# Layer 1 MLP: the seven products in another order, weights' places released a product later, chunk 1 first at the turn

## The chip, the cores and the metric

The kernel runs on one core of one Trainium2 chip. The metric is the device time of one launch in microseconds (us). A core has TensorE (matmuls, with weight loads in a lane of their own), VectorE (DVE), ScalarE (ACT), GpSimd (POOL) and SyncE (SP, which issues most transfers). Each engine takes its instructions in the order in which the program lists them, and waits at the first one whose operands are not ready.

## The reference, cut to what matters

One inference step of a small two-layer model on 640 tokens (512 latent, 128 context), width 1024. Each layer is a mixer and then an MLP with squared ReLU, whose hidden width is 4096:

```
def squared_relu_mlp(h, w1, w2):
    a = jax.nn.relu(h @ w1)
    return (a * a) @ w2
...
x = x + g2 * squared_relu_mlp(h, w_ff1[l], w_ff2[l])
```

All is float32. The change lies in the MLP of layer 1.

## The kernel before

A float32 product is made of three matmuls of reduced operands: high times high, high times low, low times high (`mm3`, lines 801 to 803). So every operand is split first: ScalarE copies the high half, and VectorE subtracts it from the value, which leaves the low half.

The MLP of layer 1 (`mlp` with `seven`) works with the tokens in two chunks of 320 (`C1`) and the hidden width in eight blocks `b` of four pieces of 128. Blocks 0 and 1 are computed plainly. For blocks 2 to 7, `blocks7` calls `up7(b, p)` twice, for the halves p = 0 and 1 of a block. A half has two pieces of the hidden width, `f` = 2p and `g` = 2p + 1. Two chunks, two halves of the 1024 rows of `w1` and two pieces form a 2x2 by 2x2 matrix product, which `up7` does with seven products in place of eight (the scheme of Strassen and Winograd). Each product is 4 x 3 matmuls of 320 columns. The token-side sums `B[0]` to `B[3]` are made once, in blocks 0 and 1 (`sums`). The weight-side sums are made on the way by `w1s_use`: the raw weights `f0, g0, f1, g1` lie in two raw tiles; for product i ScalarE and VectorE split `src` into a place (lines 558 and 559), and for some i VectorE then repairs a raw piece in place for a later product (line 563).

The seven products go to four PSUM banks, `pa`, `pd`, `pb`, `pc`; three of these are added into a second time. VectorE forms `u2 = p1 + pb` and `u3 = u2 + pd` (line 1581; `p1` is ScalarE's copy of the first `pa`, line 1598). The four results are `g` chunk 1 = `u3 + pc`, `g` chunk 0 = `u2 + pd` after its second product, `f` chunk 1 = `u2 + pc` after its second product, and `f` chunk 0 = `pa` after its second product, a plain sum without VectorE. `finish` then takes relu and square and splits the result into `aa` (lines 1586 to 1589). The program order of these steps in `up7` is written by hand.

After both halves of a block comes the turn to `down` (the product with `w2`). There `cut` first issues the groups of d = 0 and 1 for both chunks with the pieces k = 0 and 1 of the first half alone; then these groups are ended with k = 3 and 2 of the second half, and the other d follow with all four pieces. `residual` (line 1407) adds each group into `x`. Block 7 has a turn of its own with three groups of 384 columns.

The weights have eight places of 128x2x1024 in `Slots`; two are given to `B` when block 1 is done, so six remain. A `w2` piece takes a whole place, a weight of a product half of one, and a place comes back when both of its halves are released (`Weights.free`). `st.pump()` prepares the next weights of a fixed list (14 for the products of a block, then its four `w2` pieces), if a place is free, and does nothing otherwise; this puts the ScalarE copy and the VectorE subtraction (lines 214 and 216 for `w2`) at that point of both engines' program order. In the second half of a block the next weights in the list are the `w2` pieces of the same block. PSUM has six banks for this stage; a new tile takes the one that has been free longest.

Of the kernel before, what the change touches and what calls it, by code (L numbers as in the profile page):

```python
# [12 lines left out]
AF = mybir.ActivationFunctionType  # L13
ALU = mybir.AluOpType
# [122 lines left out]
class Weights:  # L137
# [118 lines left out]
    def free(self, key):  # L256
        del self.tiles[key]
        if key in self.of:
            p = self.of.pop(key)
            if isinstance(p, tuple):  # L260
                p, users, o = p
                users[0] -= 1
                if users[0] or o == 0:
                    return
            self.slots.free.append(p)
# [3 lines left out]
def body(ctx, tc, a):  # L269
    nc = tc.nc  # L270
    mm = nc.tensor.matmul
    act = nc.scalar.activation
    vec = nc.vector
# [21 lines left out]
    st = Weights(nc, rawp)  # L295
# [209 lines left out]
    def tok(t):  # L505
        return slice(t * 128, (t + 1) * 128)
# [41 lines left out]
    def w1s_use(l, b, p, i):  # L548


        def use(ts):
            if i == 0:
                fast[l, b, p] = ts
            ab, cd = (t.rearrange("p (k n) -> p k n", k=4) for t in fast[l, b, p])
            f0, g0, f1, g1 = ab[:, :, 0:128], ab[:, :, 128:256], cd[:, :, 0:128], cd[:, :, 128:256]
            src = (f0, g0, g0, f0, f1, g1, f1)[i]
            w = st.half(("w1s", l, b, p, i)).rearrange("p a (k n) -> p a k n", k=4)
            act(out=w[:, 0], in_=src, func=AF.Copy)  # L558
            vec.tensor_tensor(out=w[:, 1], in0=src, in1=w[:, 0].bitcast(F32), op=ALU.subtract)  # L559
            todo = {0: (g0, f0, g0, ALU.subtract), 1: (g0, g1, g0, ALU.subtract), 2: (f0, g0, f0, ALU.add),  # L560
                    4: (f1, f1, g0, ALU.subtract)}.get(i)
            if todo:
                vec.tensor_tensor(out=todo[0], in0=todo[1], in1=todo[2], op=todo[3])  # L563

        return use
# [197 lines left out]
    for k in range(2):  # L763
# [4 lines left out]
        out=sel, in_=ident.rearrange("p (j q) -> p q j", j=4)[:, 0:2, :], op=ALU.add, axis=AX.X  # L768
# [29 lines left out]
    def mm3(ps, st_, mv, first, last, on=False):  # L798


        mm(ps, lhsT=st_[0], rhs=mv[0], start=first, stop=False, skip_group_check=on)  # L801
        mm(ps, lhsT=st_[0], rhs=mv[1], start=False, stop=False, skip_group_check=on)  # L802
        mm(ps, lhsT=st_[1], rhs=mv[0], start=False, stop=last, skip_group_check=on)  # L803
# [79 lines left out]
    for t in range(NT):  # L883
        p = ps_kv[t][:, 0:RKV]
# [76 lines left out]
    for m in range(3):  # L961
        for c in C0:
            dst, p = qs[:, m, c[0]:c[1]], ps_qa[m, c][:, 0:c[1] - c[0]]
# [88 lines left out]
    for h in range(NH):  # L1052
        q = (new_h(f"qh{h}"), new_h(f"ql{h}"))
        Q.append(q)
        for c in C0:
            n = c[1] - c[0]
            p = psp.tile([128, 512], F32, tag="z", name="q_ps")[:, 0:n]
# [26 lines left out]
    for g in range(8):  # L1084
        p = psp.tile([128, NT, 64], F32, tag="z", name="gm_ps")
# [20 lines left out]
    for i in range(2):  # L1106
        ev = kT[i].rearrange("p (a b) n -> p a b n", b=2)
        nc.gpsimd.dma_start(
            out=ev[64:128, :, 0, :], in_=ckvT[i][64:128, 2, :].unsqueeze(1).to_broadcast([64, NH // 2, NKEY])
        )  # L1110
        nc.gpsimd.dma_start(
            out=ev[0:64, :, 1, :], in_=ckvT[i][0:64, 2, :].unsqueeze(1).to_broadcast([64, NH // 2, NKEY])
        )
    for hp_ in range(NH // 2):
        for c0 in (0, 384):
            p = psp.tile([128, 512], F32, tag="z", name="kT_ps")[:, 0:384]
# [9 lines left out]
            for e in range(2):  # L1126
                r = slice(64 * e, 64 * e + 64)
                hi, lo = (t[r, 2 * hp_ + e, c0:c0 + 384] for t in kT)
# [5 lines left out]
    for j in range(6):  # L1134
        p = psp.tile([128, 512], F32, tag="z", name="v_ps")
# [8 lines left out]
        p = p.rearrange("p (h d) -> p h d", h=NH)  # L1144
# [266 lines left out]
    def bank(nm, n):  # L1411
        return psm.tile([128, 512], F32, tag="m", name=nm)[:, 0:n]
# [34 lines left out]
    def mlp(l, C, H, lead, CL, per_d, per_c, mid, tick=None, turn=None, seven=False):  # L1447
# [107 lines left out]
        def up7(b, p):  # L1555
            n = C[0][1]

            def product(i, op, ps, first):
                w = st.need(("w1s", l, b, p, i))
                if ps is None:  # L1560
                    ps = bank("up_ps", n)
                for k in range(4):
                    r = B[op, k] if isinstance(op, int) else H[op[0]][4 * op[1] + k]
                    mm3(
                        ps, (w[:, 0, tok(k)], w[:, 1, tok(k)]), (r[:, 0, 0:n], r[:, 1, 0:n]),
                        first and k == 0, k == 3, not first,
                    )
                st.free(("w1s", l, b, p, i))
                return ps

            f, g = 2 * p, 2 * p + 1
            rs = {}
            for j in (f, g):
                A[b, j] = fa.tile([128, 2, T], F32R, tag="aa", name="aa")
                rs[j] = fr.tile([128, 2, HW], F32, tag="r", name="r").rearrange("p a n -> p (a n)")

            def new(nm):
                return sc.tile([128, 328], F32, tag="n", name=nm)[:, 0:n]

            def add(out, v, ps):  # L1580
                vec.tensor_tensor(out=out, in0=v, in1=ps, op=ALU.add)

            def finish(j, ci, src=None):
                c = slice(*C[ci])
                r, aa = rs[j][:, c], A[b, j]
                act(out=r, in_=r if src is None else src, func=AF.Relu)  # L1586
                act(out=r, in_=r, func=AF.Square)  # L1587
                act(out=aa[:, 0, c], in_=r, func=AF.Copy)  # L1588
                return lambda: vec.tensor_tensor(  # L1589
                    out=aa[:, 1, c], in0=r, in1=aa[:, 0, c].bitcast(F32), op=ALU.subtract  # L1590
                )

            def out(j, ci):
                return rs[j][:, C[ci][0]:C[ci][1]]

            pa = product(0, (0, 0), None, True)
            p1 = new("p1")
            act(out=p1, in_=pa, func=AF.Copy)
            st.pump()
            pd = product(1, 2, None, True)  # L1600
            st.pump()
            pb = product(2, 1, None, True)
            u2, u3 = new("u2"), new("u3")
            add(u2, p1, pb)
            add(u3, u2, pd)
            st.pump()
            pc = product(3, 0, None, True)
            add(out(g, 1), u3, pc)
            lo = finish(g, 1)
            st.pump()  # L1610
            pa = product(4, (0, 1), pa, False)
            lo()
            lo = finish(f, 0, pa)
            if not p:
                st.pump()
            pd = product(5, 3, pd, False)
            add(out(g, 0), u2, pd)
            lo()
            lo = finish(g, 0)
            pc = product(6, (1, 1), pc, False)  # L1620
            add(out(f, 1), u2, pc)
            lo()
            lo = finish(f, 1)
            lo()
            if not p:
                st.pump()

        def blocks7(f0):

            for b in range(NFB):  # L1630
                if b >= f0:
                    for p in range(FB // 2):
                        up7(b, p)

                cut = (lambda ds, cs: [(d, c, down(b, d, c, None, False, (0, 1))) for c in cs for d in ds])
                if b < f0:
                    for k in (2 * b, 2 * b + 1):
                        bg.add(sums(k, room(k)))
                free = (lambda h: [st.free(("w2", l, b, k, h)) for k in (0, 2)])
                if b < NFB - 1:  # L1640
                    early = cut(range(2), C) if b >= f0 else []
                    todo = [(d, c, None) for d in range(2 if early else 0, KD) for c in C]
                    for j, (d, c, ps) in enumerate(early + todo):
                        ps = down(b, d, c, ps, True, range(FB) if ps is None else (3, 2))
                        residual(ps, d, c, modc[l, 5])
                        bg.step()
                        if j == 7:
                            free(0)
                        if j % 2 or j > 3:
                            st.pump()  # L1650
                    free(1)
                    if b == f0 - 1:
                        bg.drain()
                    continue
                for c in CL:
                    early = cut(range(3), CL[0:1]) if c is CL[0] else []
                    for d in range(KD):
                        if d < len(early):
                            ps = down(b, d, c, early[d][2], True, (3, 2))
                        else:  # L1660
                            ps = down(b, d, c)
                        residual(ps, d, c, modc[l, 5])
                        per_d(c, d)
                    per_c(c)
# [36 lines left out]
        for ci in range(2):  # L1701
            i = 0
            while i < lead:
                n = WIDE[l][ci] if i == 0 else 1
                b, fs = i // FB, [(i + j) % FB for j in range(n)]
# [18 lines left out]
        f1 = lead // FB  # L1724
# [67 lines left out]
    g0 = later_h(0)  # L1792
# [276 lines left out]
    g1 = pool_vec(1)  # L2069
# [117 lines left out]
```

## Time and profile before

| | us |
|---|---|
| median of three runs | 1300.96 |
| lowest, highest | 1296.29, 1301.96 |
| the profiled execution | 1302.88 |
| its span, first to last instruction | 1301.1 |
| TensorE busy | 1261.8 |
| VectorE busy | 826.6 |
| ScalarE busy | 549.3 |

Busy is the sum of an engine's instruction times within the span. The changed code runs from about 959 us to 1265 us of the span. Matmuls overlap one another, so a matmul that lasts 0.31 us can begin 0.147 us after the one before it; a pause shows where starts lie further apart.

### The profile page before, as it was taken

What the parts mean: (1) busy time and instruction counts of PE and PEld (TensorE: products, weight loads), DVE (VectorE), ACT (ScalarE), POOL (GpSimd) and SP (SyncE); (2) the same over time, 40 slices, a digit from 0 to 9 for tenths busy, and PEclk for the clock granted to TensorE, in tenths of its full rate; (3) what the DMA queues carried; (4) which work ended last, traced back from release to release, by engine and by line L of the source; (5) the groups of instructions that cost most, each with busy time, mean ns of one, the idle gap of its engine ahead of it and who ended that gap; (6) DMA issues with size and microseconds to landing.
All of it is one profiled execution on the core that took longest, in us unless ns stands there. A gap on an engine that the chain in (4) does not pass through costs nothing.

```text
span 1301.1 us, 20746 instructions
## 1 busy us (share of the span) xinstructions
PE 1261.8 (97%) x8308; PEld 1183.4 (91%) x8308; DVE 826.6 (64%) x1553; ACT 549.3 (42%) x993; POOL 216.5 (17%) x182
## 2 busy tenths in 40 slices
PE   7999999999999999999999999799999999999997
PEld 5899975689999999999999998789999999999997
DVE  5753864564766575666666638876887567675664
ACT  4445454453453434333343414534235435354353
POOL 0010312221113221313131315610000000000001
PEclk8999999999999999999999999899999999999999
DMA  7742286340335344444353431202113223132102
GB/s 291 261 164 72 81 227 234 131 170 25 116 117 160 113 145 131 150 126 157 119 161 114 147 130 33 97 1 79 52 35 112 80 67 98 38 111 84 61 33 82
DMA packets 63200, 149.89 MB, mean 115 GB/s; under 512 B 5072, under 2 KB 21968, under 8 KB 62592
## 3 DMA queue, kind: packets, MB, share of 16 engines
q1 hardware_dynamic: 61360, 142.53, 33.3%
q0 software_dynamic: 1456, 5.96, 1.9%
q8 instruction: 65, 1.06, 0.3%
q14 instruction: 31, 0.25, 0.1%
q10 hardware_dynamic: 288, 0.08, 0.0%
HBM read 140.02 MB, written 5.39 MB: 112 GB/s over the span
## 4 chain that ended last, share of the span: by engine, by line
PE 79%; DVE 10%; ACT 7%; issue 2%; DMA 1%; POOL 0%; DVEq 0%; ACTq 0%; POOLq 0%
PE dn_ps L802 11%; PE dn_ps L801 11%; PE dn_ps L803 11%; PE up_ps L801 7%; PE up_ps L803 7%; PE up_ps L802 7%; PE wo_ps L801 1%; PE o_ps L1302 1%; PE wo_ps L803 1%; PE wo_ps L802 1%; ACT r L1587 1%; DVE w L216 1%; ACT w L558 1%; ACT r L1586 1%; PE t_ps L1269 1%
## 5 line engine op out<-in xcount | busy, mean ns | idle before, releaser
L801 PE MATMUL dn_ps<-aa,w 128*128 128x320 f32 (+4 forms) x1024 | 319.1, 312 | 2.1 <-ACT aa L1588 2.1
L802 PE MATMUL dn_ps<-aa,w 128*128 128x320 f32 (+4 forms) x1024 | 318.4, 311 | 0.7
L803 PE MATMUL dn_ps<-aa,w 128*128 128x320 f32 (+4 forms) x1024 | 316.8, 309 | 0.0
L802 PE MATMUL up_ps<-h,w 128*128 128x320 f32 (+2 forms) x800 | 248.6, 311 | 6.0 <-DVE h L752 5.9
L801 PE MATMUL up_ps<-h,w 128*128 128x320 f32 (+2 forms) x800 | 249.6, 312 | 1.3 <-ACT h L748 1.3
L803 PE MATMUL up_ps<-h,w 128*128 128x320 f32 (+2 forms) x800 | 248.6, 311 | 0.0
L1407 DVE SCALAR_TENSOR_TENSOR x<-dn_ps,mod,x 128x320 f32<-128x320 f32 (+4 forms) x360 | 144.7, 434 | 115.0 <-PE dn_ps L803 113.2
L801 PEld LDWEIGHTS dn_ps<-aa,w 128*128 128x128 f32 x1024 | 193.1, 189 | 5.8 <-ACT aa L1588 4.1
L216 DVE TENSOR_TENSOR w<-raw,w 128x1024 fp32r<-128x1024 f32 (+4 forms) x122 | 151.3, 1250 | 70.9 <-ACT w L214 69.8
L802 PEld LDWEIGHTS dn_ps<-aa,w 128*128 128x128 f32 x1024 | 193.0, 188 | 2.5 <-DVE aa L1589 2.4
L803 PEld LDWEIGHTS dn_ps<-aa,w 128*128 128x128 f32 x1024 | 193.0, 189 | 0.0
L214 ACT ACTIVATE w<-raw 128x1024 fp32r<-128x1024 f32 (+4 forms) x131 | 132.0, 1026 | 112.0 <-DMA raw<-w_ff 85.0
L802 PEld LDWEIGHTS up_ps<-h,w 128*128 128x128 f32 x800 | 151.2, 189 | 8.1 <-DVE h L752 8.1
L801 PEld LDWEIGHTS up_ps<-h,w 128*128 128x128 f32 x800 | 151.0, 189 | 4.9 <-issue 3.4
L466 POOL TENSOR_TENSOR acc<-acc,raw 128x1024 f32<-128x1024 f32 x42 | 100.7, 2399 | 303.7 <-ACT raw L464 297.6
L803 PEld LDWEIGHTS up_ps<-h,w 128*128 128x128 f32 x800 | 151.0, 189 | 0.0
L559 DVE TENSOR_TENSOR w<-raw,w 128x512 fp32r<-128x512 f32 x84 | 57.7, 687 | 34.6 <-ACT w L558 33.7
L558 ACT ACTIVATE w<-raw 128x512 fp32r<-128x512 f32 x84 | 51.4, 624 | 61.9 <-DVE raw L563 57.1
L464 ACT ACTIVATE raw<-raw,cs 128x1024 f32<-128x1024 f32 x42 | 48.3, 1149 | 62.6 <-DVE acc L459 54.2
L1925 POOL TENSOR_TENSOR y<-y,fg 128x1024 f32<-128x1024 f32 x1 | 2.4, 2392 | 416.5 <-ACT y L1921 416.5
L1481 DVE TENSOR_TENSOR r<-r,up_ps 128x328 f32<-128x328 f32 (+2 forms) x80 | 37.6, 484 | 42.6 <-ACT r L1480 41.0
L1484 DVE TENSOR_TENSOR aa<-r,aa 128x640 fp32r<-128x640 f32 (+3 forms) x52 | 39.6, 762 | 35.6 <-ACT aa L1483 35.6
(404 smaller groups left out, 2122.1 us busy)
## 6 DMA issues: line engine op xcount, KB each, us to landing
raw<-w_ff SPq DMA_DIRECT2D x126, 512.0 KB, 3.6
raw<-w_mod SPq DMA_DIRECT2D x80, 512.0 KB, 3.9
raw<-w_m SPq DMA_DIRECT2D x16, 512.0 KB, 6.0
raw<-w_out SPq DMA_DIRECT2D x8, 512.0 KB, 4.4
kT<-ckvT POOLq DMA_DIRECT2D x4, 768.0 KB, 10.8
xr<-x SPq DMA_DIRECT2D x5, 512.0 KB, 5.5
xs<-x SPq DMA_DIRECT2D x2, 1280.0 KB, 9.3
x<-xs POOLq DMA_DIRECT2D x2, 1280.0 KB, 9.6
```

The costliest lines, as they stand in the source:

```text
L214: self.nc.scalar.activation(out=w[:, 0, 0:size], in_=r, func=AF.Copy)
L216: lo.tensor_tensor(out=w[:, 1, 0:size], in0=r, in1=w[:, 0, 0:size].bitcast(F32), op=ALU.subtract)
L464: act(out=raw if k else acc[1], in_=raw, func=AF.Copy, scale=w[1])
L466: nc.gpsimd.tensor_tensor(out=acc[1], in0=acc[1], in1=raw, op=ALU.add)
L558: act(out=w[:, 0], in_=src, func=AF.Copy)
L559: vec.tensor_tensor(out=w[:, 1], in0=src, in1=w[:, 0].bitcast(F32), op=ALU.subtract)
L801: mm(ps, lhsT=st_[0], rhs=mv[0], start=first, stop=False, skip_group_check=on)
L802: mm(ps, lhsT=st_[0], rhs=mv[1], start=False, stop=False, skip_group_check=on)
L803: mm(ps, lhsT=st_[1], rhs=mv[0], start=False, stop=last, skip_group_check=on)
L1407: vec.scalar_tensor_tensor(out=xv, in0=ps[:, p0:p0 + c1 - c0], scalar=gate[:, d, m:m + 1], in1=xv, op0=ALU.mult, op1=ALU.add)
L1481: vec.tensor_tensor(out=rv, in0=rv, in1=ps, op=ALU.mult)
L1484: vec.tensor_tensor(out=aa[:, 1, lo:hi], in0=r[:, lo:hi], in1=aa[:, 0, lo:hi].bitcast(F32), op=ALU.subtract)
```

## The change

The product that adds into `pa`, the plain sum, goes from fifth to seventh place, and those on `B[3]` (into `pd`) and on chunk 1 (into `pc`) move up to fifth and sixth. `w1s_use` splits the weights in the new order, and the last repair is written to `g0` in place of `f1`. A product's weights are released after the next product has been issued (`gone`) in place of right after it. `finish` of `f` chunk 0, which reads PSUM, squares by a VectorE multiplication of the relu with the PSUM value in place of ScalarE's Square. At the end of the first half `st.pump()` becomes `st.pump(2)`. At the turn, `cut` takes chunk 1 first.

```
--- before.py
+++ after.py
@@ -553,12 +553,12 @@
                 fast[l, b, p] = ts
             ab, cd = (t.rearrange("p (k n) -> p k n", k=4) for t in fast[l, b, p])
             f0, g0, f1, g1 = ab[:, :, 0:128], ab[:, :, 128:256], cd[:, :, 0:128], cd[:, :, 128:256]
-            src = (f0, g0, g0, f0, f1, g1, f1)[i]
+            src = (f0, g0, g0, f0, g1, g0, f1)[i]
             w = st.half(("w1s", l, b, p, i)).rearrange("p a (k n) -> p a k n", k=4)
             act(out=w[:, 0], in_=src, func=AF.Copy)
             vec.tensor_tensor(out=w[:, 1], in0=src, in1=w[:, 0].bitcast(F32), op=ALU.subtract)
             todo = {0: (g0, f0, g0, ALU.subtract), 1: (g0, g1, g0, ALU.subtract), 2: (f0, g0, f0, ALU.add),
-                    4: (f1, f1, g0, ALU.subtract)}.get(i)
+                    4: (g0, f1, g0, ALU.subtract)}.get(i)
             if todo:
                 vec.tensor_tensor(out=todo[0], in0=todo[1], in1=todo[2], op=todo[3])
 
@@ -1555,6 +1555,8 @@
         def up7(b, p):
             n = C[0][1]
 
+            gone = []
+
             def product(i, op, ps, first):
                 w = st.need(("w1s", l, b, p, i))
                 if ps is None:
@@ -1565,7 +1567,10 @@
                         ps, (w[:, 0, tok(k)], w[:, 1, tok(k)]), (r[:, 0, 0:n], r[:, 1, 0:n]),
                         first and k == 0, k == 3, not first,
                     )
-                st.free(("w1s", l, b, p, i))
+
+                gone.append(("w1s", l, b, p, i))
+                if i:
+                    st.free(gone.pop(0))
                 return ps
 
             f, g = 2 * p, 2 * p + 1
@@ -1581,10 +1586,15 @@
                 vec.tensor_tensor(out=out, in0=v, in1=ps, op=ALU.add)
 
             def finish(j, ci, src=None):
+
                 c = slice(*C[ci])
                 r, aa = rs[j][:, c], A[b, j]
-                act(out=r, in_=r if src is None else src, func=AF.Relu)
-                act(out=r, in_=r, func=AF.Square)
+                if src is not None:
+                    act(out=r, in_=src, func=AF.Relu)
+                    vec.tensor_tensor(out=r, in0=r, in1=src, op=ALU.mult)
+                else:
+                    act(out=r, in_=r, func=AF.Relu)
+                    act(out=r, in_=r, func=AF.Square)
                 act(out=aa[:, 0, c], in_=r, func=AF.Copy)
                 return lambda: vec.tensor_tensor(
                     out=aa[:, 1, c], in0=r, in1=aa[:, 0, c].bitcast(F32), op=ALU.subtract
@@ -1608,22 +1618,22 @@
             add(out(g, 1), u3, pc)
             lo = finish(g, 1)
             st.pump()
-            pa = product(4, (0, 1), pa, False)
-            lo()
-            lo = finish(f, 0, pa)
-            if not p:
-                st.pump()
-            pd = product(5, 3, pd, False)
+            pd = product(4, 3, pd, False)
             add(out(g, 0), u2, pd)
             lo()
             lo = finish(g, 0)
-            pc = product(6, (1, 1), pc, False)
+            if not p:
+                st.pump()
+            pc = product(5, (1, 1), pc, False)
             add(out(f, 1), u2, pc)
             lo()
             lo = finish(f, 1)
+            pa = product(6, (0, 1), pa, False)
             lo()
+            finish(f, 0, pa)()
+            st.free(gone.pop(0))
             if not p:
-                st.pump()
+                st.pump(2)
 
         def blocks7(f0):
 
@@ -1638,7 +1648,7 @@
                         bg.add(sums(k, room(k)))
                 free = (lambda h: [st.free(("w2", l, b, k, h)) for k in (0, 2)])
                 if b < NFB - 1:
-                    early = cut(range(2), C) if b >= f0 else []
+                    early = cut(range(2), C[::-1]) if b >= f0 else []
                     todo = [(d, c, None) for d in range(2 if early else 0, KD) for c in C]
                     for j, (d, c, ps) in enumerate(early + todo):
                         ps = down(b, d, c, ps, True, range(FB) if ps is None else (3, 2))
```

## Rows read from the trace of the kernel before

**Rows 1.** The page, part 1: busy us, share of the span, instructions.
```profile
PE 1261.8 (97%) x8308; PEld 1183.4 (91%) x8308; DVE 826.6 (64%) x1553; ACT 549.3 (42%) x993; POOL 216.5 (17%) x182
```

**Rows 2.** TensorE's waits, 930 to 1301 us: total us, times, longest us.
```profile
PE up_ps L801 <- DVE u L1581: 2.4, 2, 1.5
PE dn_ps L801 <- ACT aa L1588: 2.1, 7, 0.6
```

**Rows 3.** Timeline, TensorE and weight loads: start, us, instruction, idle before and releaser.
```profile
969.86 0.42 PE L801 MATMUL up_ps<-w 128*128 128x320 f32 x1 [0.94 <-DVE u L1581]
...
983.91 0.41 PE L801 MATMUL up_ps<-w 128*128 128x320 f32 x1 [1.46 <-DVE u L1581]
...
1091.97 0.19 PEld L801 LDWEIGHTS up_ps<-w 128*128 128x128 f32 x1 [0.29 <-DVE u L1581]
...
1099.53 0.42 PE L801 MATMUL dn_ps<-aa,w 128*128 128x320 f32 x1 [0.25 <-ACT aa L1588]
```

**Rows 4.** Timeline, TensorE: first matmuls of block 3 and of block 4's halves.
```profile
1016.59 0.31 PE L801 MATMUL up_ps<-h,w 128*128 128x320 f32 x1
...
1070.65 0.31 PE L801 MATMUL up_ps<-h,w 128*128 128x320 f32 x1
...
1082.98 0.31 PE L801 MATMUL up_ps<-h,w 128*128 128x320 f32 x1
```

**Rows 5.** Timeline, VectorE in block 4.
```profile
1077.44 0.49 DVE L1581 TENSOR_TENSOR u<-u,up_ps 128x320 f32<-128x320 f32 x1
1077.85 0.68 DVE L559 TENSOR_TENSOR w<-raw,w 128x512 fp32r<-128x512 f32 x1
1078.45 0.48 DVE L1581 TENSOR_TENSOR r<-u,up_ps 128x320 f32<-128x320 f32 x1
1080.99 0.69 DVE L559 TENSOR_TENSOR w<-raw,w 128x512 fp32r<-128x512 f32 x1 [2.06 <-ACT w L558]
1081.72 0.69 DVE L563 TENSOR_TENSOR raw<-raw 128x512 f32<-128x512 f32 x1
...
1088.64 2.36 DVE L216 TENSOR_TENSOR w<-raw,w 128x1024 fp32r<-128x1024 f32 x2 [0.58 <-ACT w L214]
1090.92 0.48 DVE L1581 TENSOR_TENSOR u<-p,up_ps 128x320 f32<-128x320 f32 x1
1091.43 0.49 DVE L1581 TENSOR_TENSOR u<-u,up_ps 128x320 f32<-128x320 f32 x1
```

**Rows 6.** Timeline, ScalarE in block 4.
```profile
1078.96 0.47 ACT L1586 ACTIVATE r<-r 128x320 f32<-128x320 f32 x1 [1.28 <-DVE r L1581]
...
1079.97 0.47 ACT L1588 ACTIVATE aa<-r 128x320 fp32r<-128x320 f32 x1
1080.35 0.61 ACT L558 ACTIVATE w<-raw 128x512 fp32r<-128x512 f32 x1
...
1086.72 0.61 ACT L558 ACTIVATE w<-raw 128x512 fp32r<-128x512 f32 x1
1087.24 0.42 ACT L1598 ACTIVATE p<-up_ps 128x320 f32<-128x320 f32 x1
1087.56 2.94 ACT L214 ACTIVATE w<-raw 128x1024 fp32r<-128x1024 f32 x3
```

**Rows 7.** Timeline, TensorE behind two long pauses of other stages.
```profile
814.79 1.42 PE L718 MATMUL R_ps<-ones,sq 128*128 128x1 f32 x7 [4.10 <-DVE sq L707]
...
844.30 0.41 PE L802 MATMUL up_ps<-h,w 128*128 128x320 f32 x1 [2.50 <-DVE h L752]
...
845.93 0.47 PE L803 MATMUL up_ps<-h,w 128*128 128x320 f32 x1
...
849.13 0.35 PE L803 MATMUL up_ps<-h,w 128*128 128x320 f32 x1
```

**Rows 8.** Windows: stretch, length, each engine's busy us, granted clock, DMA share, GB/s.
```profile
816.00:817.00 1.00, 1.00 (x7) 1.00 (x6) 0.00 (x0) 0.00 (x0) 1.00 (x2) 0.50 0.82 295
...
846.00:848.00 2.00, 2.00 (x9) 2.00 (x8) 1.46 (x4) 0.62 (x2) 0.00 (x0) 0.50 0.00 0
```


## What the change will do

> **What bounds the kernel now.** I read the page first. TensorE is busy 97% of the span [rows 1], so a change of order can only win or lose time in which TensorE stands still. The chain of waits from 930 us to the end comes next. In this stretch the changed code runs, and there TensorE waits for two things that the diff touches: for `u`, the sums that VectorE makes out of the products, and at the turn for the high half of an activation [rows 2]. The timeline then shows where. In block 2, the first with seven products, the sixth product of each half waits for `u` (0.94 and 1.46 us); in later blocks only that of the second half does (0.29); and the turn, where `down` takes over, waits 0.25 for `aa` [rows 3].
>
> How much that is per block follows from three starts. Block 3 begins at 1016.59 and block 4 at 1070.65, a period of 54.06 us [rows 4]. The first half of block 4 takes 12.33 us for 84 matmuls, 0.147 each or 1.76 a product [rows 4]. A block has 2x84 matmuls in the products and 16x12 in `down`, 360 in all, which at this pace are 52.8 us. So a block loses 1.2 us: 0.3 at the sixth product of the second half, and 0.9 at the turn (the wait and the slow restart behind it).
>
> Why is `u` late? VectorE and ScalarE take their work in program order and hand it to and fro. In block 4, `u3` starts at 1077.44 in the first half and at 1091.43 in the second [rows 5], 13.99 us apart, though seven products take only 12.33. In block 2, where both are waited for, the sixth products restart 14.05 apart [rows 3]. The chain of VectorE and ScalarE, not TensorE, sets this interval, and the slack built up in the first half hides most of it. Ahead of `u2` and `u3` in the second half stand two splits of a `w2` block, 1.14 us each on VectorE (1088.64 to 1090.92) [rows 5], behind three ScalarE copies that begin at 1087.56 [rows 6].
>
> **The change part by part.**
>
> *The bank with `u3`'s operand comes one product earlier.* The product on `B[3]` adds into the bank `pd`, which `u3` must have read. It was the sixth, it is the fifth. In the first half of block 4 the fifth product is due at 1070.65 + 4x1.76 = 1077.69 [rows 4]. `u3` starts at 1077.44 [rows 5], and from the start of `u3` to the restart it takes 0.54 (1091.43 to 1091.97) [rows 3, 5], so it can begin at 1077.98: a new wait of 0.3. Before, it had one product more of room.
>
> *The chain from `u3` to the next `u3`.* This is what decides, and I lay it end to end. Up to the repair of the raw weights (1081.72) nothing in front changes: 4.28 us [rows 5]. Then follow, in the new program order, with steps from start to start out of the rows: `g` chunk 0 is added (0.60 behind a 128x512 operation on VectorE, 1077.85 to 1078.45); relu on ScalarE (0.51, the hand-over 1078.45 to 1078.96); square and high half (1.01, 1078.96 to 1079.97); high half of the next weights (0.38, 1079.97 to 1080.35); their low half on VectorE (0.64, 1080.35 to 1080.99); `f` chunk 1 is added behind it (0.60); relu, square, high half (0.51 + 1.01); its low half (0.51); the new multiplication of `f` chunk 0 (0.41, as 1077.44 to 1077.85); its high half on ScalarE (0.51); weights of the seventh product (0.38); the first `w2` copy, which the new `pump(2)` brings here (0.52, 1086.72 to 1087.24); `p1` (0.97, a third of the triple at 1087.56); the second `w2` copy (0.32, 1087.24 to 1087.56); its split on VectorE (1.08, 1087.56 to 1088.64); the third split (1.14); `u2` (1.14); `u3` (0.51) [rows 5, 6]. The sum is 17.0 us, against 13.99 now. What makes it longer: the low half of weights stands between the two sums of the first half, `f` chunk 0 comes after all the others, and `w2` splits that stood behind `u3` stand ahead of it.
>
> *The wait in the second half.* When the fifth product of the first half has waited for `u3`, that of the second is due 12.33 later, and its `u3` comes 17.0 later: 4.7 us of wait. The bound from below is 0, if the splits do not stand ahead of `u3` (a rival below). From above, `u3` could also carry the two further hand-overs that I let overlap, 1.0 more. I take 4.7, since each step stands in the rows of one block.
>
> *Places released a product later.* No copy into a place waits for TensorE inside the products of block 4, so this gains nothing there. There are six places for weights. I counted takes and releases in the new order. When the weights of the second half's seventh product have their place, at the end of the first half, two places are free: the first and the second `w2` copy get them. The third gets the one that comes back after the second product, and the fourth stays behind the fourth product, as now. So `pump(2)` is not refused, and the splits move ahead. A copy less stands after `u2`. The first three `w2` loads are issued on SP's queue in the stage before; the fourth follows the low half of the seventh weights, some 6 us ahead of its copy in my chain. I cost the transfers at nothing.
>
> *Squares.* Twelve ScalarE squares (0.50 a step) become twelve VectorE multiplications that read PSUM, like the sums (0.48 for the sum at 1078.45) [rows 5]. They are in the chain above. The other target of the repair changes no step.
>
> *The turn.* Chunk 1 comes first and is ready early; `f` chunk 0 is needed 39 matmuls after the last product (four groups of six, then fifteen), 5.7 us, and its chain of relu, multiplication, high and low half is four hand-overs of 0.51, 2.0 us. I cost the wait at the turn at nothing: 0.9 a block is gained. If VectorE still works off the second half's queue, half of this returns.
>
> *The sum.* Blocks 3 to 6 each: 0.3 + 4.7 - 1.2 = +3.8, together 15.2. Block 2: its waits of 0.94, 1.46 and 0.9 (3.3) become 0.94 + 1.76 = 2.7 and 4.7: +4.1. Block 7: 0.3 + 4.7, less 0.3 and less its turn, the longest one (0.6 us of wait [rows 2], which I estimate at 1.7 with two restarts): +3.0. In all +22.3 us.
>
> **The clock.** After 4.10 us without a matmul (to 814.79) the granted clock is 0.50 at 816 to 817, the lower level of 1.2 GHz; after 2.50 us (to 844.30, behind other pauses) it is 0.50 as well [rows 7, 8]. In the second case twelve matmuls from 845.93 to 849.13 take 0.267 each in place of 0.147: 1.4 us lost [rows 7]. The 1.46 us wait of today is shorter than either. Waits of 4.7 us are longer than both, so I add 6 x 1.4 = 8.5 us. The Trainium skill (TensorE: Matmul & The Clock Gate, Part 1: The HAM clock gate) says that half rate is the array's default and that only activity releases it, so a pause gives the clock back; the two rows agree, and by the rule the sum is +31, without it +22.
>
> The profiled execution took 1302.88 us (span 1301.1), 1.9 above the median of 1300.96. I add the difference to the median: 1300.96 + 22.3 + 8.5 = 1332.
>
> **Rivals.**
> - *The waits come, the clock stays.* 1300.96 + 22.3 = 1323, between 1315 and 1328 as the chain is 1 us shorter or longer in six blocks. For it: the pause at 844 had shorter ones in front, and one after 4.10 us is a single case. Chance 0.26.
> - *Not slower: the places run out.* If `pump(2)` and the pump after the first product find no free place, the `w2` splits go behind `u3`. My chain stands at 11.35 us when the weights of the seventh product are copied; from there VectorE would go to their low half (0.64), `u2` (0.60) and `u3` (0.51): 13.1. It decides at 13.2: 12.33 plus the 0.9 that the turn pays back. The time is 1301, between 1296 and 1306. Against it: the three copies that run back to back at 1087.56 show three places free by then, and by my count two of them are so already where the new order asks. Chance 0.12.
> - *Faster: all waits vanish.* If ScalarE and VectorE overlapped where I add hand-overs, some 11 us of waits could go: 1290. The 14.05 of block 2 speaks against it, as that interval is made of just such steps. Chance 0.04.
> - *The clock stays low for longer*, twice 1.4 us at each wait, or falls in the first half of block 2 too: 1342 and more. Chance 0.08.
>
> **How the numbers follow.** The forecast has 0.50, 1325 to 1342 by itself. With the first rival it holds 0.76; the range 1313 to 1342 adds the shorter chains. Left out are the two cases at or below today's time (0.16) and the longest one. A difference under 0.5% (6.5 us) can't be told from none in this kernel. Slower by more: 0.50 + 0.26 + 0.08 and a little of the place rival, 0.85. The same: 0.10, most of that rival. Faster: 0.05.
>
> **What the profile after would show.** TensorE's waits for `u` at the product sums: twelve, the six of second halves between 4 and 5.5 us, together some 28 to 32 us, in place of 2.4. The wait for `aa` at the turn gone or under 0.3. In the timeline of ScalarE a `w2` copy ahead of `p1`, and on VectorE two `w2` splits between the last low half and `u2`. The interval of `u3` to `u3` inside a block at 16 to 18 us. The granted clock at 0.50 shortly after each long wait. The prediction is wrong if the `w2` splits stand behind `u3`, if the interval stays near 14, or if the clock stays at 1.0, which takes 8.5 us off.

## The result and the profile after

The changed kernel takes 1335.19 us (median of four runs, 1333.27 to 1337.55), the kernel before in the same comparison 1301.46 (1296.29 to 1303.79). The ratio is 1.0266, with a 95% interval of 1.0231 to 1.0301: slower by 33.7 us. The forecast was 1332.

| | before | after |
|---|---|---|
| the profiled execution, us | 1302.88 | 1333.27 |
| its span | 1301.1 | 1330.5 |
| TensorE busy | 1261.8 | 1268.5 |
| VectorE busy | 826.6 | 832.8 |
| ScalarE busy | 549.3 | 544.7 |

The page of the kernel after, part 1, answers to [rows 1]: the same number of matmuls, and a share of the span that has fallen from 97% to 95%.

```profile
PE 1268.5 (95%) x8308; PEld 1195.2 (90%) x8308; DVE 832.8 (63%) x1565; ACT 544.7 (41%) x981; POOL 216.4 (16%) x182
```

The chain of waits of the kernel after, TensorE from 930 us to the end (total us, times, longest us), answers to [rows 2]. The wait for `u` has gone from 2.4 us in two places to 28.4 in twelve. The wait for `aa` at the turn (2.1 us in seven) is no longer in the list.

```profile
PE up_ps L801 <- DVE u L1586: 28.4, 12, 4.3
PE up_ps L801 <- DVE x L1407: 0.4, 1, 0.4
```

Where they lie, in the timeline of TensorE (start, us, instruction, idle before and releaser), answers to [rows 3, 4]:

```profile
965.60 0.45 PE L801 MATMUL up_ps<-w 128*128 128x320 f32 x1 [2.71 <-DVE u L1586]
...
982.65 0.39 PE L801 MATMUL up_ps<-w 128*128 128x320 f32 x1 [2.92 <-DVE u L1586]
...
1042.09 0.60 PE L801 MATMUL up_ps<-w 128*128 128x320 f32 x1 [4.33 <-DVE u L1586]
...
1078.18 0.31 PE L801 MATMUL up_ps<-h,w 128*128 128x320 f32 x1
...
1085.60 0.38 PE L801 MATMUL up_ps<-w 128*128 128x320 f32 x1 [0.23 <-DVE u L1586]
...
1102.50 0.60 PE L801 MATMUL up_ps<-w 128*128 128x320 f32 x1 [4.33 <-DVE u L1586]
1102.90 0.47 PE L802 MATMUL up_ps<-w 128*128 128x320 f32 x1
...
1137.50 0.31 PE L801 MATMUL up_ps<-h,w 128*128 128x320 f32 x1
```

The first two lines are block 2, the third the second half of block 3. 1078.18 and 1137.50 are the first matmuls of blocks 4 and 5, 59.32 us apart, where a block took 54.06. In block 4 the fifth product of the first half waits 0.23 us, that of the second half 4.33.

Why `u` is late stands in VectorE's timeline of block 4, the answer to [rows 5]. The steps from `u3` (second of a pair of sums) to the next `u3`:

```profile
1084.96 0.49 DVE L1586 TENSOR_TENSOR u<-u,up_ps 128x320 f32<-128x320 f32 x1
...
1095.32 0.48 DVE L1594 TENSOR_TENSOR r<-r,up_ps 128x320 f32<-128x320 f32 x1
...
1096.86 0.69 DVE L559 TENSOR_TENSOR w<-raw,w 128x512 fp32r<-128x512 f32 x1
1097.81 3.62 DVE L216 TENSOR_TENSOR w<-raw,w 128x1024 fp32r<-128x1024 f32 x3 [0.26 <-ACT w L214]
1101.35 0.48 DVE L1586 TENSOR_TENSOR u<-p,up_ps 128x320 f32<-128x320 f32 x1
1101.87 0.49 DVE L1586 TENSOR_TENSOR u<-u,up_ps 128x320 f32<-128x320 f32 x1
```

`u3` comes 16.91 us after `u3` (1084.96 to 1101.87), where seven products take 12.33. Directly ahead of the sums stand three splits of `w2` pieces, back to back, where [rows 5] had two. Line 1594 is the new multiplication. ScalarE's timeline of the same stretch, the answer to [rows 6], shows a `w2` copy at 1096.73 ahead of `p1` (1097.68):

```profile
1096.21 0.62 ACT L558 ACTIVATE w<-raw 128x512 fp32r<-128x512 f32 x1
1096.73 1.04 ACT L214 ACTIVATE w<-raw 128x1024 fp32r<-128x1024 f32 x1
1097.68 0.41 ACT L1608 ACTIVATE p<-up_ps 128x320 f32<-128x320 f32 x1
1098.00 1.99 ACT L214 ACTIVATE w<-raw 128x1024 fp32r<-128x1024 f32 x2
```

Windows of the kernel after around the pause that ends at 1042.09 (stretch, length, each engine's busy us, granted clock, DMA share, GB/s) answer to [rows 8]:

```profile
1040.00:1042.00 2.00, 0.00 (x0) 0.00 (x0) 1.91 (x3) 0.00 (x0) 0.00 (x0) 0.73 0.68 206
1042.00:1044.00 2.00, 1.91 (x7) 1.94 (x8) 0.49 (x1) 1.37 (x4) 0.00 (x0) 0.50 1.00 293
1044.00:1046.00 2.00, 2.00 (x10) 2.00 (x9) 0.98 (x1) 0.99 (x2) 0.00 (x0) 0.50 0.85 299
1046.00:1048.00 2.00, 2.00 (x10) 2.00 (x10) 1.04 (x3) 1.26 (x3) 0.00 (x0) 0.56 0.35 70
1048.00:1050.00 2.00, 2.00 (x15) 2.00 (x14) 0.89 (x2) 1.12 (x4) 0.00 (x0) 1.00 0.54 209
```

Here the granted clock falls before the pause is over (0.73 in a window without a matmul), and behind it stands at the lower of its two levels, 1.2 GHz: TensorE is busy all the time there, with ten matmuls in a window of two microseconds where the last window has fifteen. The Trainium skill (TensorE: Matmul & The Clock Gate, Part 1: The HAM clock gate) calls half rate the default, which only activity releases; these rows agree, 0.50 behind the pause and 1.00 in the last window.

**The stretch.** The rows that follow compare kernels by one measure: the time from the first matmul of block 2's products to the first of block 7's `down`. It holds the changed code and no difference of the stages in front. (The turn of block 7 lies behind it: from its first matmul to its last it takes 34.02 us before and 31.92 after, 2.1 less.) A matmul of 320 columns counts as slow when the next one starts 0.25 to 0.28 us after it in place of 0.147, in a row of three or more such. Worked out from the starts in TensorE's timeline:

```
kernel          stretch  periods: 2->3   3->4   4->5   5->6   6->7   slow matmuls
before          298.47          57.39  54.06  54.00  54.02  54.03     0
after           334.07          62.65  60.47  59.32  60.28  59.27   101
filler          322.32          61.14  57.91  57.85  57.85  57.86     0
one_pump        326.66          61.71  58.50  58.43  58.34  58.20    88
order_only      324.89          61.62  58.40  58.34  58.35  58.21    77
rest_only       315.78          60.44  57.07  56.78  57.12  57.03    50
after_behind    299.73          57.98  54.02  53.96  53.97  53.98    12
behind_sums     290.75          54.80  52.81  ...                     0
best            290.72          54.77  52.82  ...                     0
```

### The profile page after: what moved, and what is told of

Read it like the earlier page. It is cut to its first block, busy times and chain, and to the rows that moved or that the text cites. A ratio compares the mean times of both kernels' runs of the same rounds, so it can differ in the third digit from the quotient of the medians.

```text
span 1330.5 us, 20765 instructions
## 1 busy us (share of the span) xinstructions
PE 1268.5 (95%) x8308; PEld 1195.2 (90%) x8308; DVE 832.8 (63%) x1565; ACT 544.7 (41%) x981; POOL 216.4 (16%) x182
## 4 chain that ended last, share of the span: by engine, by line
PE 78%; DVE 12%; ACT 6%; DMA 2%; issue 2%; POOL 0%; DVEq 0%; ACTq 0%; POOLq 0%
PE dn_ps L801 11%; PE dn_ps L802 11%; PE dn_ps L803 11%; PE up_ps L801 8%; PE up_ps L802 8%; PE up_ps L803 8%; DVE w L559 2%; ACT w L558 1%; PE wo_ps L801 1%; PE o_ps L1302 1%; PE wo_ps L802 1%; PE wo_ps L803 1%; PE mod_ps L344 1%; PE t_ps L1269 1%; DVE raw L563 1%
## 5 line engine op out<-in xcount | busy, mean ns | idle before, releaser
L1407 DVE SCALAR_TENSOR_TENSOR x<-dn_ps,mod,x 128x328 f32<-128x328 f32 (+5 forms) x360 | 144.6, 434 | 127.8 <-PE dn_ps L803 126.8
L802 PEld LDWEIGHTS up_ps<-h,w 128*128 128x128 f32 x800 | 153.9, 192 | 6.7 <-DVE h L752 6.6
L801 PEld LDWEIGHTS up_ps<-h,w 128*128 128x128 f32 x800 | 153.9, 192 | 4.9 <-issue 3.4
L803 PEld LDWEIGHTS up_ps<-h,w 128*128 128x128 f32 x800 | 153.3, 192 | 0.0
```

What stands on the lines that cost most here:

```text
L1407: vec.scalar_tensor_tensor(out=xv, in0=ps[:, p0:p0 + c1 - c0], scalar=gate[:, d, m:m + 1], in1=xv, op0=ALU.mult, op1=ALU.add)
```

## Experiments

The theory: the order of VectorE's and ScalarE's work puts `u3` 17 us behind `u3`, TensorE waits for it once a half, and each long pause also costs the clock. The rivals: the clock costs nothing, so that the waits are the whole; the late release of places holds up the weights; the loss is not the order of the products but one of the other edits.

### The clock apart from the waits: filler

The kernel after, with matmuls that nobody reads ahead of the fifth product of each second half (24) and of block 2's first half (12). They fill the pause; the sums come no earlier.

```
+            def fill(m):
+                ps = psa.tile([128, 512], F32, tag="a", name="fill_ps")[:, 0:n]
+                w = st.tiles["w1s", l, b, p, 3]
+                for _ in range(m):
+                    mm(ps, lhsT=w[:, 0, tok(0)], rhs=B[0, 0][:, 0, 0:n], start=True, stop=True)
...
             st.pump()
+            if p or b == 2:
+                fill(24 if p else 12)
             pd = product(4, 3, pd, False)
```

> The changed kernel with idle matmuls put into its two kinds of long pause: 24 (3.5 us) ahead of the fifth product of every second half, 12 (1.8 us) ahead of that of block 2's first half; they write a PSUM bank that nobody reads. Theory (the pause lets the clock fall, and the slow matmuls behind it are a cost of their own): the granted clock stays at 1.00 in this stage, some 118 matmuls get back 0.12 us each, 14 us, and the second pause of block 2 grows by 1.4: 1322 us, with the same starts of u3. Rival (the slow matmuls come with the wait whatever TensorE does, or they cost nothing as VectorE would make TensorE wait anyway): within 2 us of the changed kernel, 1333 to 1337.

Measured: 1322.43 us (1317.81 to 1324.05) against 1299.69 before; 1.0168 (1.0135 to 1.0201). TensorE's waits in its chain of waits:

```profile
PE up_ps L801 <- DVE u L1586: 7.2, 12, 1.0
```

The pause in block 4's second half, in TensorE's timeline:

```profile
1096.83 1.33 PE L1610 MATMUL fill_ps<-h,w 128*128 128x320 f32 x8
...
1098.97 0.39 PE L801 MATMUL up_ps<-w 128*128 128x320 f32 x1 [0.81 <-DVE u L1586]
1099.19 0.31 PE L802 MATMUL up_ps<-w 128*128 128x320 f32 x1
```

The windows around the pause of block 3's second half:

```profile
1039.00:1041.00 2.00, 1.30 (x9) 1.03 (x8) 1.94 (x3) 0.00 (x0) 0.00 (x0) 1.00 0.80 219
1041.00:1043.00 2.00, 1.88 (x13) 1.91 (x14) 0.49 (x1) 1.34 (x4) 0.00 (x0) 1.00 0.97 313
1043.00:1045.00 2.00, 2.00 (x15) 2.00 (x14) 0.94 (x1) 1.03 (x2) 0.00 (x0) 1.00 0.81 280
```

The fifth product still waits for `u`, now 0.81 us behind the last filler, so the sums and not TensorE set its start, and they come no earlier: the fifth products of block 4 restart 16.90 us apart in both kernels (1082.07 to 1098.97 here, 1085.60 to 1102.50 in the kernel after). The clock stays at 1.00, there is no slow matmul in the stretch, and the stretch is 334.07 - 322.32 = 11.75 us shorter. This kernel has more work and is faster, by the clock alone. The rest, 322.32 - 298.47 = 23.9 us, is waits.

### Which edit: the new order alone, and the rest alone

order_only is the kernel before with the new order in `w1s_use` and in the tail of `up7`, and nothing else: ScalarE's square, release at once, one pump at the half's end, chunk 0 first.

```
-            src = (f0, g0, g0, f0, f1, g1, f1)[i]
+            src = (f0, g0, g0, f0, g1, g0, f1)[i]
...
-            pa = product(4, (0, 1), pa, False)
-            lo()
-            lo = finish(f, 0, pa)
-            if not p:
-                st.pump()
-            pd = product(5, 3, pd, False)
+            pd = product(4, 3, pd, False)
...
+            pa = product(6, (0, 1), pa, False)
             lo()
+            finish(f, 0, pa)()
```

> The kernel before with the new order of the products alone: release at once, one weight preparation, ScalarE's Square, chunk 0 first. Theory (the new order alone brings the bank of u3 a product earlier and makes the hand-overs longer): pauses of 0.3 and 3.3 us and 1.0 at the turn, +3.4 a block or +20, and the clock falls behind the long one, +8 to +12: 1330 us. Rival (the order is harmless, the other parts cost): 1300 to 1306.

Measured: 1325.45 us (1323.79 to 1326.82); 1.0196 (1.0174 to 1.0218). The chain of waits of order_only:

```profile
PE up_ps L801 <- DVE u L1581: 22.3, 12, 3.3
```

and `u3` and the next `u3` in VectorE's timeline of block 4:

```profile
1082.57 0.49 DVE L1581 TENSOR_TENSOR u<-u,up_ps 128x320 f32<-128x320 f32 x1
...
1098.43 0.49 DVE L1581 TENSOR_TENSOR u<-u,up_ps 128x320 f32<-128x320 f32 x1
```

Three quarters of the loss come with the order alone: twelve waits at the same places, the long ones a microsecond shorter than after the whole change. A wait at the turn did not come, although chunk 0 is first here; that part of the expectation was wrong. So the wait at the turn goes without chunk 1 first.

rest_only is the kernel after with the old order: late release, `pump(2)`, the multiplication and chunk 1 first stay.

```
-            src = (f0, g0, g0, f0, g1, g0, f1)[i]
+            src = (f0, g0, g0, f0, f1, g1, f1)[i]
...
-            pd = product(4, 3, pd, False)
-            add(out(g, 0), u2, pd)
+            pa = product(4, (0, 1), pa, False)
             lo()
-            lo = finish(g, 0)
+            lo = finish(f, 0, pa)
...
```

> The changed kernel with the old order of the products: release a product later, two weight preparations, the multiplication in place of Square for f chunk 0, chunk 1 first. Theory: the sixth product waits 2.4 us for u3 in second halves, and the turn about 1.2, as f chunk 1 is last again and now first wanted; +2.4 a block, +14; a pause of 2.4 us lies between the 1.5 that kept the clock and the 2.7 that lost it, so 0 to 8 more: 1316 to 1324. Rival (only the order matters): 1300 to 1304.

Measured: 1318.49 us (1316.2 to 1319.14); 1.0140 (1.0118 to 1.0162). Its chain of waits:

```profile
PE up_ps L801 <- DVE u L1586: 14.4, 7, 2.2
...
PE dn_ps L801 <- ACT aa L1598: 0.9, 2, 0.6
```

The rest costs 18.8 us by itself, the order 25.8, together 33.7: the parts do not add up. Both lengthen the same interval. From `u3` to `u3` in block 4 it is 13.99 us before, 15.86 in order_only (1082.57 to 1098.43), 16.38 in rest_only (1082.77 to 1099.15) and 16.91 after. The rest lengthens it more than the order does, yet waits less, because the product that needs `u3` is still the sixth there: its first halves keep a product's time of slack (1.76 us), and the order is what takes it. In numbers, 16.38 less 12.33 less 1.76 is 2.3 us, and the pauses are of 2.2; in order_only 15.86 less 12.33 is 3.5, and the pauses are of 3.3. The turn of rest_only, expected to wait about 1.2 us, waits 0.6 in two blocks only. The pauses of rest_only showed something else. Two ends of pauses in TensorE's timeline, of nearly the same length:

```profile
1042.66 0.42 PE L801 MATMUL up_ps<-w 128*128 128x320 f32 x1 [2.25 <-DVE u L1586]
...
1099.69 0.41 PE L801 MATMUL up_ps<-w 128*128 128x320 f32 x1 [2.23 <-DVE u L1586]
```

and the windows behind each:

```profile
1044.00:1046.00 2.00, 2.00 (x10) 2.00 (x9) 0.32 (x1) 1.94 (x4) 0.00 (x0) 0.52 1.01 339
...
1101.00:1103.00 2.00, 2.00 (x15) 2.00 (x15) 0.29 (x1) 1.97 (x4) 0.00 (x0) 1.00 1.01 348
```

The first pause was followed by a clock of 0.52, the second by 1.00.

### The places and the second pump: free_now, one_pump

free_now is the kernel after with the release put back right behind each product:

```
-                gone.append(("w1s", l, b, p, i))
-                if i:
-                    st.free(gone.pop(0))
+                st.free(("w1s", l, b, p, i))
...
-            st.free(gone.pop(0))
```

> The changed kernel with the places released at once, as before. Theory (no copy of weights waits for a place on the path of u3; only the fourth w2 piece moves): 1334 us, within 2 of the changed kernel. Rival (the late release is what keeps the pieces back or frees ScalarE): 4 us or more away from it, either way.

Measured: 1335.01 us (1334.78 to 1335.3); 1.0265 (1.0237 to 1.0294), with 28.5 us of waits for `u` in twelve places, the longest 4.3. That is the kernel after. The late release holds up nothing, and gains nothing.

one_pump is the kernel after with one pump at the end of the first half:

```
-                st.pump(2)
+                st.pump()
```

> The changed kernel with a single weight preparation at the end of the first half, as before, in place of two. Theory (the chain from u3 to u3 is a sum of steps in program order): one w2 copy (0.97) leaves the path ahead of p1, so the interval is 1 us shorter and the pause in second halves 3.4 in place of 4.3 us; six times 0.9 is 5.5 us, and the clock still falls: 1329 us. Rival (the w2 splits ahead of the sums are the whole cause): the pause goes to about 0.3 and the time to 1305.

Measured: 1326.64 us (1321.41 to 1327.88); 1.0198 (1.0169 to 1.0227). Its chain of waits:

```profile
PE up_ps L801 <- DVE u L1586: 22.8, 12, 3.4
```

The second pump moves one more `w2` split (1.14 us a step) ahead of `u2`, and makes the interval 16.91 us where it is 15.96 in one_pump (1082.64 to 1098.60). By the medians that is 8.6 us (1335.19 less 1326.64), by the stretch 7.4: a microsecond of wait in each second half, and some of the clock.

### The splits ahead of the sums: behind_sums, after_behind

If the splits ahead of `u2` and `u3` are what makes the second halves late, they must be worth something in the kernel before too. behind_sums is the kernel before, without the two pumps that stand ahead of the sums in second halves; the `w2` pieces are then prepared by the later pumps.

```
-            st.pump()
+            if not p:
+                st.pump()
             pd = product(1, 2, None, True)
-            st.pump()
+            if not p:
+                st.pump()
```

> The kernel before with one edit: in second halves the weight preparations behind the first and second product are left out, so that the w2 splits come behind u2 and u3 (two there, two in the stage of down). Theory (two w2 splits ahead of u2 set the wait of the sixth product and, through VectorE's queue, that of the turn): u3 to u3 falls from 14 to about 12 us, the waits of blocks 3 to 7 vanish and most of block 2's second half: -8 us, 1293. Rival (a w2 piece is then late for down, and TensorE waits there): 1301 or more.

Measured: 1292.83 us (1291.47 to 1294.23) against 1301.17; 0.9941 (0.9917 to 0.9964). VectorE's timeline in block 4:

```profile
1070.13 0.49 DVE L1581 TENSOR_TENSOR u<-u,up_ps 128x320 f32<-128x320 f32 x1
...
1081.22 0.49 DVE L1581 TENSOR_TENSOR u<-p,up_ps 128x320 f32<-128x320 f32 x1 [0.47 <-PE up_ps L803]
1081.74 0.49 DVE L1581 TENSOR_TENSOR u<-u,up_ps 128x320 f32<-128x320 f32 x1
1082.14 1.22 DVE L216 TENSOR_TENSOR w<-raw,w 128x1024 fp32r<-128x1024 f32 x1
```

`u3` to `u3` is 11.61 us here, less than the 12.33 of seven products. VectorE now waits for TensorE (0.47 ahead of `u2`), and the split stands behind the sums. A block takes 52.81 us, the 360 matmuls at 0.147 and nothing else. The longest that are left in its chain of waits are one for `u` in block 2 and one for a low half of `w2` in block 7:

```profile
PE dn_ps L803 <- DVE w L216: 1.5, 1, 1.5
PE up_ps L801 <- DVE u L1581: 1.0, 1, 1.0
```

after_behind is the kernel after with the same edit, and one pump at the end of the first half:

```
-            st.pump()
+            if not p:
+                st.pump()
             pd = product(1, 2, None, True)
-            st.pump()
+            if not p:
+                st.pump()
...
-                st.pump(2)
+                st.pump()
```

> The changed kernel with the same edit and a single preparation at the end of the first half; order, late release, multiplication and chunk 1 first stay. Theory: pauses of 0.3 and 0.6 us a block, none at the turn, no fall of the clock except behind block 2's first pause: 1300 to 1304 us. Rival (the new order costs by itself, since pd is wanted a product earlier): 1320 or more.

Measured: 1303.12 us (1298.74 to 1306.2); 1.0017 (0.9998 to 1.0036). Its chain of waits:

```profile
PE up_ps L801 <- DVE u L1586: 6.1, 11, 2.7
PE dn_ps L803 <- DVE w L216: 1.5, 1, 1.5
PE dn_ps L801 <- ACT aa L1598: 0.7, 1, 0.7
```

With the splits out of the way the kernel is within 2 us of the one before. But the same edit is worth 8.3 us there too, so what stays of the change shows against behind_sums: 10.3 us by the medians. By the traces 3.2 of it lie in block 2, 1.15 in each of blocks 3 to 7 up to block 7's turn (53.97 against 52.82 a block, together 5.8), and 1.3 in that turn (35.10 against 33.81 from its first matmul to its last), where the wait for `aa` is new. How much of this is the order's and how much that of the multiplication, the late release and chunk 1 first, which stay in, is not shown. In blocks 3 to 7 each half still waits, 0.23 to 0.47 us. The interval in block 4 is 13.02 us (1076.78 to 1089.80), 0.7 above what seven products take. So the change, less the second pump, still costs 10 us where no `w2` split stands ahead of the sums, and 27 where two do (one_pump).

### Three edits alone on the kernel before: pump2_only, chunk1_only, mult_only

pump2_only:

```
             if not p:
-                st.pump()
+                st.pump(2)
```

> The kernel before with two weight preparations at the end of the first half in place of one, nothing else. Theory: a third w2 split stands ahead of u2, the sixth product of second halves waits 1.1 to 1.3 in place of 0.3 us, but the fourth split leaves the path to the turn, which then waits for nothing; -0.1 to +0.3 a block: 1299 to 1303 us, no change. Rival (this is the edit that costs): 1306 or more.

Measured: 1301.19 us (1295.91 to 1303.93) against 1301.62; 0.9998 (0.9982 to 1.0015). Its chain of waits:

```profile
PE up_ps L801 <- DVE u L1581: 8.1, 7, 2.2
```

There is no wait at the turn any more. The second halves wait a microsecond for `u`, and the turn's loss is gone: the same time, in another place.

chunk1_only:

```
-                    early = cut(range(2), C) if b >= f0 else []
+                    early = cut(range(2), C[::-1]) if b >= f0 else []
```

> The kernel before with chunk 1 first at the turn, nothing else. Theory: f chunk 1, the last result of the old order, is then wanted 1.8 us sooner; the turn waits 1.8 in place of 0.9 us in blocks 2 to 6: +4.5, 1305 us, no fall of the clock. Rival (the order of chunks is free as four groups cover the turn): 1301.

Measured: 1306.04 us (1300.52 to 1309.17); 1.0027 (1.0009 to 1.0045). Its chain of waits:

```profile
PE dn_ps L801 <- ACT aa L1588: 6.8, 7, 1.2
```

In the old order `f` chunk 1 is the last result, and chunk 1 first waits 1.2 us for it in place of 0.25. In the new order no run shows a use of this edit either: order_only has chunk 0 first, and its turn waits for nothing.

mult_only:

```
-                act(out=r, in_=r if src is None else src, func=AF.Relu)
-                act(out=r, in_=r, func=AF.Square)
+                if src is not None:
+                    act(out=r, in_=src, func=AF.Relu)
+                    vec.tensor_tensor(out=r, in0=r, in1=src, op=ALU.mult)
+                else:
+                    act(out=r, in_=r, func=AF.Relu)
+                    act(out=r, in_=r, func=AF.Square)
```

> The kernel before with the multiplication in place of Square for f chunk 0, nothing else. Theory: in the old order f chunk 0 stands in the middle of the chain, and a step on ScalarE (0.5) becomes two hand-overs to VectorE and back behind its queue; the sixth product waits 1.6 in place of 0.3 us and the turn 1.2 in place of 0.9: +1.7 a block, 1308 to 1312 us. Rival (it unloads ScalarE): 1299 or less.

Measured: 1309.78 us (1306.84 to 1314.61); 1.0071 (1.0044 to 1.0098). Its chain of waits:

```profile
PE up_ps L801 <- DVE u L1581: 10.5, 7, 2.2
...
PE dn_ps L801 <- ACT aa L1592: 4.5, 7, 1.0
```

A square on ScalarE follows its relu on the same engine. The multiplication on VectorE adds two hand-overs in the middle of the chain, and the second halves then wait 1.5 us for `u`.

### The version that beats both: best

behind_sums, and in block 7 two pumps after the products of the second half, for the low half of `w2` that was late there:

```
             if not p:
                 st.pump()
+            elif b == NFB - 1:
+                st.pump(2)
```

> The kernel before with the w2 splits of second halves behind the sums (the run of that name), and in block 7 the two left-over w2 pieces prepared right behind the products. Theory: the only wait that this left behind block 2, 1.5 us for a low half of w2 in block 7's down, goes: 1291 us. Rival (the two splits delay the residuals there): 1293 or more.

Measured: 1290.33 us (1287.39 to 1291.64) against 1301.62; 0.9915 (0.9897 to 0.9933). What its chain of waits still holds in the stretch and behind it:

```profile
PE up_ps L801 <- DVE u L1581: 0.9, 1, 0.9
PE up_ps L801 <- DVE x L1407: 0.5, 1, 0.5
PE y_ps L1948 <- ACT y L1959: 0.3, 1, 0.3
```

The wait of 1.5 us in block 7 is gone. Whether that second edit is worth anything in device time is not shown: the intervals of best and behind_sums overlap.

## Why the prediction was right, and where not

- **The bank of `u3` one product earlier: right.** Forecast 0.3 us in first halves, measured 0.23.
- **The chain from `u3` to `u3`: right in cause and size.** Forecast 17.0 us laid end to end, measured 16.91. Three `w2` splits stand ahead of `u2`; the sign that named two of them was one short. Of the 2.92 us that the change adds to the interval, 1.87 come with the order (15.86 in order_only against 13.99) and 0.95 with the second pump (16.91 against 15.96 in one_pump), which leaves 0.1 for the three other edits, each taken on top of the one before. The `w2` splits are the part that can be moved: taken away, the interval falls to 11.61 us in the old order and to 13.02 in the new.
- **The wait in second halves: right in five of six.** Forecast 4.7, measured 4.33 of idle time. The idle time leaves out the slow restart, and by the period the term is exact: with the clock kept, a block takes 57.86 us in filler against 54.03, +3.83 where +3.8 was forecast. Block 2's second pause was 2.92 and not 4.7. Its fifth products restart 17.05 us apart (965.60 to 982.65), about as in the other blocks (16.90); but its first pause had cost the clock, thirteen slow matmuls in between made TensorE 1.6 us later, and it had that much less to wait. Clock time lost between two waits of one chain is not paid twice. I had left that out.
- **Waits in all.** The stretch lost 23.9 us to waits, and the turn of block 7 gives back 2.1: 21.8, where 22.3 was forecast.
- **Late release, transfers, turn: right.** free_now equals the kernel after; the wait at the turn is gone. That chunk 1 first is what removes it is not borne out: it is gone in order_only too, with chunk 0 first.
- **The clock: right in cause, the term mis-sized.** The step "so I add 6 x 1.4 = 8.5 us" took twelve slow matmuls behind each pause from one case in [rows 7] (and 6 x 1.4 is 8.4). In the runs of slow matmuls there were 13, 12, 19, 11, 18, 10 and 18, behind seven pauses: 101 x 0.12 = 12.1 us, less the 1.6 that block 2 hides, is 10.5. filler measured 11.75. Most of the difference is the first step behind a pause of 4.33 us: at the lower clock the second matmul starts 0.40 us after the first (1102.50 to 1102.90), in filler 0.22 (1098.97 to 1099.19), or 0.9 us in five blocks. Block 2's first pause, 2.71 us, cost the clock too. The prediction gave that pause 2.7 us, and in [rows 7] one of 2.50 had cost the clock, so by its own rows it was to be counted; only the last rival had allowed for it.
- **The sum.** 21.8 + 11.75 = 33.6 us, against 33.7 measured and 31 forecast. The clock's term was about 3 us short, and that of the waits 0.5 too long.
- **The rivals.** That the clock stays is ruled out by filler. That the places run out is ruled out by the three splits ahead of `u2`. That all waits vanish was wrong for this change, though the time that it named, 1290, is that of best: it is to be had from the splits' place, not from the products' order. That the clock stays low for longer came in part: three of the five pauses of 4.33 us were followed by 18 or 19 slow matmuls and not by twelve.

## What to carry to other kernels

When a product moves up in an order written by hand, lay the other engines' work from one use of its bank to the next end to end, hand-overs included, and compare the sum with the time of the matmuls in between: the difference is the wait, in every round. Work that is not yet needed (here the `w2` splits) belongs behind the sums that TensorE waits for, and where it is issued can matter more than the order of the products. When a pause can't be avoided, the clock behind it is a second cost, a third of the loss here; matmuls that nobody reads win that part back.

## What was not expected of the hardware

The clock is not a plain matter of a pause's length. Of eight pauses of 2.2 us in the stretch, five were followed by a run of slow matmuls and three were not: four of six in rest_only, the one in pump2_only, not the one in mult_only. Two of 1.92 and 1.97 us, in block 2 of order_only and one_pump, were followed by one, though they were shorter; both came 13 us behind a pause of 2.7 us that had already cost the clock once, and whether that matters is not shown. None of those of 1.0 to 1.5 us was (mult_only has five of 1.43 to 1.50), and each of 2.7 us and more that no filler covered was. The run behind pauses of 4.33 us was not of one length either: 19, 11, 18, 10 and 18 matmuls, which shows in the periods of the kernel after as 60.47, 59.32, 60.28 and 59.27. So a single case of a clock loss, like that of [rows 7], sizes the term only within a factor of two.
